# Fixed order on TensorE in the attention, later transposes, and the gains of q, k and v inside the split of their weights

## Chip, cores and metric

One core of one Trainium2 chip runs the whole program in one launch. The metric is the device time in microseconds (us) of an execution; the median of three runs of the kernel before is 1498.02 us (1497.49 to 1499.73). All data are float32, and the result is compared with a float32 reference.

## The reference

A trunk of two layers on 512 tokens of width 1024: a gated short convolution with its feed-forward part, then dilated attention with its own. The attention is what matters here. Keys and values come from a normalised stream with a gain of its own (`kv_norm`), queries from the same stream with `mix_norm_pre[1]`:

```
q = rope(rms_norm(x, mix_norm_pre[1]) @ w_q)       # 3 branches x 16 heads x 64
k, v = rms_norm(h, kv_norm) @ w_kv                 # the same split; k gets rope
for g, (window, dilation) in enumerate(((128, 1), (512, 4), (2048, 16))):
    s = (q_g / 8) @ k_g.T, masked to t, t-d, ..., t-window
    o_g = softmax(s) @ v_g ; lse_g = logsumexp(s)
o = sum_g softmax_g(lse) * o_g ; y = o @ w_o
```

## The kernel before, in words

Every large product is made of three matmuls on parts in a short float format: a weight w is split into `wh` (w rounded by ScalarE, `nc.scalar.copy` in `split`, L93) and `wl` (w minus `wh`, by VectorE, L94), an activation likewise into `xh`, `xl` (`zh`, `zl` are the same tiles seen in the attention's order), and `wh·xh + wl·xh + wh·xl` is summed in a PSUM bank. PSUM has eight banks, four with the tag "mm" and four with the tag "at". Weights arrive as 1 MB loads (L101, SyncE's queue, two `raw` tiles); a load gives two pairs of split tiles, and there are six tiles of each kind. For q, k and v the gain of the norm belongs to the rows of the weight, so `parts` first multiplies `raw` by it in place (L113, VectorE, two products for each half of a load) and then splits.

The attention goes through the 16 heads in four groups of four (`for i in range(NG)`, L758). A group has two stages.

- The q and k projections (`rope_mms`, L543): six loads, each a `feature_mm` of 48 matmuls of 512 columns into two "mm" banks, followed by `rope` (L527): eight ScalarE copies of 32x512 into two tiles of the pool "t" (four tiles), and three VectorE products for each bank. After each load `fill()` takes two pending pieces of work (L553).
- The v projections (`values`, L645): three loads in two pieces of 48 matmuls of 256 columns, and after each piece `fill()` again takes two.

What `fill` takes in the v stage are the scores (`scores`, L577): eight calls for two parts (branch 0; branches 1 and 2 together), two pairs of heads and two halves of the blocks. A call opens two "at" banks, and its matmuls use 64 rows of the array, rows 0 to 63 for one head of the pair and 64 to 127 for the other. VectorE adds the mask and takes the maximum (L597), ScalarE takes the exponential (L607). Then `factors` (L610) exchanges the sums of the two parts through DMAs on GpSimd's queue and makes one factor for each row. What `fill` takes in the following group's q and k stage are the units (L730): `transposed` (L676) scales p by its factor (VectorE, L685), transposes it into two "at" banks (L688) and lets ScalarE copy it into two tiles of the pool "t" (L690). One unit later `times_v` (L693) multiplies it with v into an "at" bank that two heads share (64 columns of the array each); the last one of a pair of heads copies that bank out on ScalarE (`O`, L726) or splits it into `xh`, `xl`. The last group's units stand between the first matmuls of the output projection (`wo_step`, L513; L781 to L784).

A planner with a simulated timeline makes each engine's order. It takes what is ready and was written first, gives out tiles of a pool as they are given back, and adds the waits. `tc.issue_after(m)` binds an instruction to come behind `m` on the same engine; before the change that is used in the attention only behind the first product with v (L716).

Of the kernel before, what the change touches and what calls it, by code (L numbers as in the profile page):

```python
# [7 lines left out]
F32 = mybir.dt.float32  # L8
# [30 lines left out]
def trunk(  # L39
# [64 lines left out]
    def parts(src, gain=None, pool=wp, bufs=6):  # L104

        _, a, b = src.shape
        wh = pool.tile([P, a, b], F32R, tag="wh", name="wh", bufs=bufs, align_bytes=LINE)
        wl = pool.tile([P, a, b], F32R, tag="wl", name="wl", bufs=bufs, align_bytes=LINE)
        if gain is not None:
            for i in range(0, a, a // 2):  # L110
                ks = slice(i, i + a // 2)
                g = gain[:, ks].rearrange("p (a x) -> p a x", x=1)
                nc.vector.tensor_tensor(  # L113
                    src[:, ks], src[:, ks], g.broadcast_to([P, a // 2, b]), ALU.mult)
        split(wh, wl, src)
        return wh, wl

# [4 lines left out]
    def feature_mm(jobs, t0, t1, attn):  # L122
# [28 lines left out]
    def feature_mms(makers, between=None, attn=False, marks=((),) * 4):  # L151
# [5 lines left out]
        if between is None:  # L157
            pairs = [m() for m in makers]
            for i in range(0, len(pairs), 2):
                feature_mm(pairs[i:i + 2], 0, NT, attn)  # L160
# [14 lines left out]
    def makers(tag, raw, gain=None):  # L175

        return [lambda j=j: (bank(tag, tag + "f"), parts(raw[:, :, j * P:(j + 1) * P], gain))
                for j in range(2)]

    def token_mm(outs, ah, al, wh, wl, first, last):  # L180

        for i, o in enumerate(outs):
# [330 lines left out]
    def wo_step(k, tt, n):  # L513
        wh, wl = ws[4 * n + k // 2]
        return token_mm([ys[tt][n]], xh[:, tt, k, :], xl[:, tt, k, :],
                        [wh[:, k % 2, :]], [wl[:, k % 2, :]], k == 0, k == KT - 1)

    with ExitStack() as inner:
# [24 lines left out]
        def rope_mms(g, i, rest, fill):  # L543
# [4 lines left out]
            for src, gain in ((w_q[0], gq), (w_kv, gkv)):  # L548
                tag = "at" if ms and rest else "mm"
                ms += makers(tag, load_cols(src, c0), gain)  # L550
                if not rest:
                    d += [rope(ps, f"qk{g}", g) for ps in feature_mms(ms[-2:], None, True)]
# [9 lines left out]
        class Heads:  # L562
# [14 lines left out]
            def scores(self, part, pr, b2):  # L577

                st = self.st[part]
                ps = [bank("at", "s").rearrange("p (b k) -> p b k", b=2) for _ in range(2)]  # L580
                for b in (b2, b2 + 1):
                    for e in range(2):
# [4 lines left out]
                        for h2 in range(2):  # L587
                            rw = slice(64 * h2, 64 * h2 + 64)
                            nc.tensor.matmul(  # L589
                                ps[h2][:, b - b2, e * P:(e + 1) * P],  # L590
                                q[pr][rw, b * P:(b + 1) * P], k[pr][rw, kb * P:(kb + 1) * P],
                                start=True, stop=True)
                    lo = 128 if part == 0 and b == 0 else 0
                    mask = (maskA, maskB)[part]
                    for h2 in range(2):
                        hh = 2 * pr + h2
                        nc.vector.tensor_tensor_reduce(  # L597
                            self.p(part, hh, b), ps[h2][:, b - b2, lo:], mask[:, lo:],
                            1.0, -3.0e38, ALU.add, ALU.max, st[:, b, hh, 0:1])
                if b2 == 0:  # L600
                    return
# [43 lines left out]
            def values(self, g):  # L645

                raw = load_cols(w_kv, QW + g * NH * HD + self.i * 256)
                w = [parts(raw[:, 4 * j:4 * j + 4, :], gkv[:, 4 * j:4 * j + 4]) for j in range(2)]
# [4 lines left out]
                def piece(n):  # L653
                    for k in range(KT):
                        wh, wl = (x[:, k % 4, :] for x in w[k // 4])
                        for p in range(3):
                            for m in range(2):
                                nc.tensor.matmul(  # L658
                                    ps[m][:, n, :], (zh, zh, zl)[p][:, k, 2 * m + n],
                                    (wh, wl, wh)[p],  # L660
                                    start=k == 0 and p == 0, stop=k == KT - 1 and p == 2)
# [14 lines left out]
            def transposed(self, pr, part, hh, b2):  # L676
# [5 lines left out]
                for b in (b2, b2 + 1):  # L682
# [4 lines left out]
                    for e in range(lo, 256, P):  # L687
                        nc.tensor.transpose(  # L688
                            tr[:, b - b2, e:e + P], p[:, e - lo:e - lo + P], ident)
# [3 lines left out]
            def times_v(self, pr, part, b2, trs):  # L693
# [5 lines left out]
                mark = None  # L699
                for b in (b2, b2 + 1):  # L700
                    for e in range(2):
                        if part == 0 and b + e == 0:
                            continue
                        for hh in range(2):
# [11 lines left out]
                            with tc.issue_after(mark) if mark else nullcontext():  # L716
                                m = nc.tensor.matmul(  # L717
# [146 lines left out]
```

## Time and profile before

| what | value |
|---|---|
| median of three runs | 1498.02 us |
| profiled execution | 1498.81 us, span 1497.0 us |
| TensorE (PE) | 1484.5 us busy, 99% |
| weight loads on TensorE (PEld) | 1256.2 us, 84% |
| VectorE (DVE) | 741.6 us, 50% |
| ScalarE (ACT) | 615.6 us, 41% |
| GpSimd (POOL) | 58.2 us, 4% |
| mean granted TensorE clock | 0.999 |
| HBM read, written | 133.92 MB, 2.23 MB |

An instruction's time runs from its start to its modelled end; matmuls overlap, so the distance from one start to the next is what one costs in a row of them. A run is what stands in one line of the timeline: instructions of one kind without another between them. One score matmul or product with v of the code is two instructions in the trace, one transpose is one.

### The profile page before, as it was taken

To read this page: it belongs to the slowest core of one execution; us is meant where nothing else is said; L and a number is where in the kernel's file an instruction comes from. 1 tells how busy PE (TensorE), PEld (TensorE's weight loads), DVE (VectorE), ACT (ScalarE), POOL (GpSimd) and SP (SyncE) were. 2 spreads that over 40 slices of the span, in tenths; PEclk is the share of its full clock that TensorE was granted. 3 is DMA by queue.
4 is the path that set the end of the run, shared out by engine and by line. 5 is a ranking of instruction groups with operands and counts; after the bars stand their busy time and mean duration, and the time that the engine had idled before them with its cause. 6 is when DMAs were issued, how large, how long until landed. Compare 5 with 4: busy or idle time off the path is not lost.

```text
span 1497.0 us, 19969 instructions
## 1 busy us (share of the span) xinstructions
PE 1484.5 (99%) x8155; PEld 1256.2 (84%) x8155; DVE 741.6 (50%) x1312; ACT 615.6 (41%) x1133; POOL 58.2 (4%) x108
## 2 busy tenths in 40 slices
PE   9999999999999999999999999999999999999998
PEld 8888898888888889898788889889879888888886
DVE  5735453323233368767667566765546332323332
ACT  5313342212123236574666557466554221212321
POOL 1000100000000020000001001000010000000000
PEclk9999999999999999999999999999999999999999
DMA  6343033223323303222122212212123322332311
GB/s 219 107 141 109 33 113 113 72 98 113 123 88 113 113 29 113 85 86 86 57 65 79 85 64 81 85 57 86 31 85 113 113 71 98 113 124 87 113 57 56
DMA packets 110369, 137.43 MB, mean 92 GB/s; under 512 B 3485, under 2 KB 99013, under 8 KB 110278
## 3 DMA queue, kind: packets, MB, share of 16 engines
q1 hardware_dynamic: 108708, 135.56, 27.2%
q8 instruction: 64, 1.05, 0.3%
q0 software_dynamic: 1280, 0.26, 0.2%
q10 hardware_dynamic: 290, 0.33, 0.1%
q14 instruction: 27, 0.22, 0.0%
HBM read 133.92 MB, written 2.23 MB: 91 GB/s over the span
## 4 chain that ended last, share of the span: by engine, by line
PE 66%; issue 26%; DMA 3%; DVE 2%; POOL 1%; ACT 1%; POOLq 0%; DVEq 0%; SPq 0%; ACTq 0%
PE mmf L140 26%; PE atf L140 14%; PE vps L658 8%; PE s L589 2%; PE o L717 2%; PE tr L688 2%; DMA raw<-in_w_kv 1%; DVE raw L113 1%; DMA raw<-in_ffn_w_gate_up 1%; POOL y L207 1%; DMA raw<-in_w_q 1%; DVE wl L94 1%; POOL a L205 1%; PE y1b L187 0%; PE y1a L183 0%
## 5 line engine op out<-in xcount | busy, mean ns | idle before, releaser
L94 DVE TENSOR_TENSOR wl<-raw,wh 128x1024 fp32r<-128x1024 f32 x244 | 292.9, 1222 | 74.6 <-ACT wh L93 74.2
L93 ACT CAST wh<-raw 128x1024 fp32r<-128x1024 f32 x244 | 246.8, 1047 | 104.3 <-PE atf L140 42.7
L140 PE MATMUL mmf<-xh,wh 128*128 128x512 f32 (+1 forms) x848 | 275.2, 377 | 2.8 <-ACT xh L93 2.8
L140 PE MATMUL mmf<-xl,wh 128*128 128x512 f32 (+1 forms) x848 | 271.4, 374 | 0.0
L140 PE MATMUL mmf<-xh,wl 128*128 128x512 f32 (+1 forms) x848 | 270.7, 374 | 0.0
L140 PE MATMUL atf<-xh,wh 128*128 128x512 f32 (+1 forms) x560 | 181.0, 365 | 0.0
L140 PE MATMUL atf<-xl,wh 128*128 128x512 f32 (+1 forms) x560 | 180.1, 365 | 0.0
L140 PE MATMUL atf<-xh,wl 128*128 128x512 f32 (+1 forms) x560 | 180.0, 365 | 0.0
L140 PEld LDWEIGHTS mmf<-xh,wh 128*128 128x128 f32 x848 | 152.8, 188 | 32.5 <-ACT xh L93 3.5
L366 DVE TENSOR_TENSOR act<-atf,s 128x512 f32<-128x512 f32 x44 | 30.4, 692 | 301.6 <-ACT s L365 301.6
L140 PEld LDWEIGHTS mmf<-xl,wh 128*128 128x128 f32 x848 | 153.3, 188 | 28.7 <-issue 0.9
L140 PEld LDWEIGHTS mmf<-xh,wl 128*128 128x128 f32 x848 | 153.3, 188 | 27.9
L365 ACT ACTIVATE s<-mmf 128x512 f32<-128x512 f32 x44 | 26.3, 598 | 334.9 <-PE mmf L140 326.7
L113 DVE TENSOR_TENSOR raw<-raw,cols 128x512 f32<-128x512 f32 x144 | 90.4, 686 | 85.7 <-DMA raw<-in_w_kv 60.5
L140 PEld LDWEIGHTS atf<-xl,wh 128*128 128x128 f32 x560 | 99.5, 189 | 16.9
L140 PEld LDWEIGHTS atf<-xh,wl 128*128 128x128 f32 x560 | 99.5, 189 | 17.0
L140 PEld LDWEIGHTS atf<-xh,wh 128*128 128x128 f32 x560 | 99.6, 188 | 16.6
L536 ACT COPY sw<-mmf 32x512 f32<-32x512 f32 x92 | 53.3, 579 | 78.7 <-PE mmf L140 71.4
L658 PE MATMUL vps<-wh,xh 128*128 128x256 f32 x384 | 81.2, 289 | 0.0
L658 PE MATMUL vps<-wh,xl 128*128 128x256 f32 x384 | 79.3, 286 | 0.0
L658 PE MATMUL vps<-wl,xh 128*128 128x256 f32 x384 | 79.1, 285 | 0.0
L94 DVE TENSOR_TENSOR al<-act,ah 128x512 fp32r<-128x512 f32 x44 | 30.2, 691 | 96.4 <-ACT ah L93 96.4
(182 smaller groups left out, 1993.6 us busy)
## 6 DMA issues: line engine op xcount, KB each, us to landing
raw<-in_ffn_w_gate_up SPq DMA_DIRECT2D x44, 1024.0 KB, 6.6
raw<-in_w_kv SPq DMA_DIRECT2D x24, 1024.0 KB, 5.2
raw<-in_ffn_w_down SPq DMA_DIRECT2D x22, 1024.0 KB, 4.8
raw<-in_w_q SPq DMA_DIRECT2D x12, 1024.0 KB, 5.2
raw<-in_conv_w_in SPq DMA_DIRECT2D x11, 1024.0 KB, 5.1
raw<-in_conv_w_out SPq DMA_DIRECT2D x4, 1024.0 KB, 4.8
raw<-in_w_o SPq DMA_DIRECT2D x4, 1024.0 KB, 5.0
h<-in_x SPq DMA_DIRECT2D x4, 512.0 KB, 7.1
```

Of the source, the lines that this page charges most:

```text
L93: return [nc.scalar.copy(hi, src).ins, nc.vector.tensor_tensor(lo, src, hi.bitcast(F32), ALU.subtract).ins]
L94: nc.vector.tensor_tensor(lo, src, hi.bitcast(F32), ALU.subtract).ins]
L113: nc.vector.tensor_tensor(src[:, ks], src[:, ks], g.broadcast_to([P, a // 2, b]), ALU.mult)
L140: nc.tensor.matmul(ps, (wh, wl, wh)[p][:, k, :], x[p == 2][:, k], start=i == 0, stop=i == len(todo) - 1)
L205: nc.gpsimd.tensor_scalar(a, ssq[:, 0:1], EPS, ssq[:, 1:2], ALU.add, ALU.add)
L365: nc.scalar.activation(s, ps[2 * j], AF.Silu)
L366: nc.vector.tensor_tensor(act[2 * c + j], ps[2 * j + 1], s, ALU.mult)
L536: nc.scalar.copy(w[s:s + 32], y[s + 32:s + 64])
L589: nc.tensor.matmul(ps[h2][:, b - b2, e * P:(e + 1) * P], q[pr][rw, b * P:(b + 1) * P], k[pr][rw, kb * P:(kb + 1) * P], start=True, stop=True)
L658: nc.tensor.matmul(ps[m][:, n, :], (zh, zh, zl)[p][:, k, 2 * m + n], (wh, wl, wh)[p], start=k == 0 and p == 0, stop=k == KT - 1 and p == 2)
L688: nc.tensor.transpose(tr[:, b - b2, e:e + P], p[:, e - lo:e - lo + P], ident)
L717: m = nc.tensor.matmul(out, v, rhs, start=first, stop=part == 0 and e == 1, skip_group_check=True).ins
```

## The change

The diff does three things. `strict` ties each of the attention's matmuls (q and k but for the first load pair, scores, v, transposes, products with v, the first 24 steps of the output projection) behind the one traced before it. The scores are four calls in place of eight, with four "at" banks each; `fill` takes one piece of work, before a v piece, and in a q or k load in the middle of its matmuls and behind its rope; the units come after three empty ones (but for the last group), and products with v of two units stand together. And `parts` with a gain makes `wh` by a ScalarE multiplication with a factor for each partition and `wl` by one VectorE instruction, one of each for each of the weight's 128-row slices, on half a load of 256 columns (`gained`); the product in place is gone.

```diff
     def parts(src, gain=None, pool=wp, bufs=6):
...
-        if gain is not None:
-            for i in range(0, a, a // 2):
-                ks = slice(i, i + a // 2)
-                g = gain[:, ks].rearrange("p (a x) -> p a x", x=1)
-                nc.vector.tensor_tensor(
-                    src[:, ks], src[:, ks], g.broadcast_to([P, a // 2, b]), ALU.mult)
-        split(wh, wl, src)
+        if gain is None:
+            split(wh, wl, src)
+            return wh, wl
+        for i in range(a):
+            g = gain[:, i:i + 1]
+            nc.scalar.mul(wh[:, i], src[:, i], g)
+            nc.vector.scalar_tensor_tensor(
+                wl[:, i], src[:, i], g, wh[:, i].bitcast(F32), ALU.mult, ALU.subtract)
         return wh, wl
 
+    def gained(raw, gain):
+        return [parts(raw[:, k:k + 4], gain[:, k:k + 4]) for k in (0, 4)]
...
+    traced = []
+    def strict(op, *args, **kwargs):
+        with tc.issue_after(traced[0]) if traced else nullcontext():
+            traced[:] = [op(*args, **kwargs).ins]
...
         for i, (k, p) in enumerate(todo):
-            for ps, (_, (wh, wl)) in zip(outs, jobs):
-                nc.tensor.matmul(ps, (wh, wl, wh)[p][:, k, :], x[p == 2][:, k],
-                                 start=i == 0, stop=i == len(todo) - 1)
+            if fill and i == len(todo) // 2:
+                fill()
+            for ps, (_, w) in zip(outs, jobs):
+                args = ps, w(p == 1, k), x[p == 2][:, k]
+                kwargs = {"start": i == 0, "stop": i == len(todo) - 1}
+                if fill:
+                    strict(nc.tensor.matmul, *args, **kwargs)
+                else:
+                    nc.tensor.matmul(*args, **kwargs)
...
-            def scores(self, part, pr, b2):
+            def scores(self, part, pr):
                 st = self.st[part]
-                ps = [bank("at", "s").rearrange("p (b k) -> p b k", b=2) for _ in range(2)]
-                for b in (b2, b2 + 1):
+                banks = [[bank("at", "s").rearrange("p (b k) -> p b k", b=2) for _ in range(2)]
+                         for _ in range(2)]
+                for b in range(NT):
...
-                w = [parts(raw[:, 4 * j:4 * j + 4, :], gkv[:, 4 * j:4 * j + 4]) for j in range(2)]
+                w = gained(raw, gkv)
...
-                def unit(pr, part, b2):
-                    self.flight.append(((pr, part, b2), [
-                        self.transposed(pr, part, hh, b2) for hh in (2 * pr, 2 * pr + 1)]))
-                    if len(self.flight) > 1:
+                def unit(n, what):
+                    if n % 2 == 0:
                         self.rest()
-                return [lambda a=(pr, part, b2): unit(*a)
-                        for pr in range(2) for part in (1, 0) for b2 in (0, 2)] + [self.rest]
+                    if what:
+                        pr, part, b2 = what
+                        self.flight.append((what, [
+                            self.transposed(pr, part, hh, b2) for hh in (2 * pr, 2 * pr + 1)]))
+                whats = [(pr, part, b2) for pr in range(2) for part in (1, 0) for b2 in (0, 2)]
+                return [lambda a=a: unit(*a) for a in enumerate(whats + [None])]
 
             def rest(self):
-                what, trs = self.flight.pop(0)
-                self.times_v(*what, trs)
+                for what, trs in self.flight:
+                    self.times_v(*what, trs)
+                self.flight.clear()
...
         def fill():
-            for f in todo[:2]:
-                f()
-            del todo[:2]
+            if todo:
+                todo.pop(0)()
...
-            todo = [lambda a=(part, pr, b2): heads.scores(*a)
-                    for part in range(2) for pr in range(2) for b2 in (0, 2)]
+            todo += [lambda a=(part, pr): heads.scores(*a)
+                     for part in range(2) for pr in range(2)]
             for g in range(NB):
                 for piece in heads.values(g):
+                    fill()
                     piece()
-                    fill()
             heads.factors()
-            todo = heads.units()
+            todo += [lambda: None] * (3 if i < NG - 1 else 0) + heads.units()
...
-        for n, f in enumerate(todo):
+        for n, f in enumerate(list(todo)):
             for s in steps[3 * n:3 * n + 3]:
-                wo_step(*s, 0)
+                wo_step(*s, 0, True)
             f()
```

## Rows read from the trace of the kernel before

**Rows 1.** Busy time by stretch: engines, granted clock, DMA share, GB/s.

```profile
624.90:673.60 48.70, 48.48 (x409) 44.80 (x408) 34.58 (x103) 35.06 (x98) 3.51 (x6) 1.00 0.28 88
673.60:756.50 82.90, 82.90 (x471) 66.93 (x470) 55.06 (x110) 45.14 (x76) 2.61 (x5) 1.00 0.23 72
756.50:803.90 47.40, 47.40 (x410) 44.30 (x409) 33.19 (x101) 34.42 (x97) 3.90 (x7) 1.00 0.25 78
803.90:885.90 82.00, 82.00 (x471) 66.64 (x470) 53.83 (x109) 45.13 (x75) 1.97 (x4) 1.00 0.24 75
...
1015.30:1062.80 47.50, 47.50 (x409) 44.16 (x408) 25.71 (x87) 36.78 (x100) 4.56 (x8) 1.00 0.22 75
1062.80:1101.40 38.60, 37.42 (x271) 29.46 (x269) 16.31 (x56) 15.91 (x30) 1.31 (x3) 1.00 0.09 29
```

**Rows 2.** Timeline of TensorE in a V stage: start, duration, instructions.

```profile
762.00 0.40 PE L658 MATMUL vps<-wh,xl 128*128 128x256 f32 x2
762.33 0.94 PE L589 MATMUL s<-qk,qk 64*128 64x128 f32 x12
763.20 0.50 PE L658 MATMUL vps<-wh,xh 128*128 128x256 f32 x2
763.54 0.39 PE L658 MATMUL vps<-wl,xh 128*128 128x256 f32 x2
...
777.35 1.16 PE L589 MATMUL s<-qk,qk 64*128 64x128 f32 x16
778.44 0.50 PE L658 MATMUL vps<-wh,xl 128*128 128x256 f32 x2
```

**Rows 3.** Timeline of TensorE in the QK stages.

```profile
690.43 0.61 PE L140 MATMUL mmf<-xh,wl 128*128 128x512 f32 x2
...
694.96 0.62 PE L140 MATMUL mmf<-xl,wh 128*128 128x512 f32 x2
...
815.25 1.91 PE L688 MATMUL tr<-ident,p 128*128 128x128 f32 x16
816.92 0.71 PE L140 MATMUL mmf<-xh,wl 128*128 128x512 f32 x2
...
825.72 1.09 PE L717 MATMUL o<-trs,v 128*64 128x128 f32 x16
826.75 0.73 PE L140 MATMUL mmf<-xl,wh 128*128 128x512 f32 x2
...
869.70 0.88 PE L717 MATMUL o<-trs,v 128*64 128x128 f32 x12
870.51 0.50 PE L140 MATMUL mmf<-xh,wh 128*128 128x512 f32 x1
```

**Rows 4.** Timeline of ScalarE behind two projections.

```profile
744.39 0.58 ACT L536 COPY sw<-mmf 32x512 f32<-32x512 f32 x1 [4.10 <-PE mmf L140]
...
749.13 2.00 ACT L93 CAST wh<-raw 128x1024 fp32r<-128x1024 f32 x2
751.15 0.59 ACT L726 COPY O<-o 128x512 f32<-128x512 f32 x1
...
819.51 2.00 ACT L93 CAST wh<-raw 128x1024 fp32r<-128x1024 f32 x2
821.53 1.08 ACT L690 COPY trs<-tr 128x512 f32<-128x512 f32 x2
```

**Rows 5.** Groups by line and shape: count, busy, mean ns, idle before.

```profile
L93 ACT CAST wh<-raw 128x1024 fp32r<-128x1024 f32 x244 | 246.8, 1047 | 104.3 <-PE atf L140 42.7 <-issue 14.0 <-DMA raw<-in_ffn_w_gate_up 14.0
L607 ACT ACTIVATE p<-p,nm 128x256 f32<-128x256 f32 x112 | 55.3, 496 | 11.7 <-DVE nm L604 9.9 <-DMA d<-st 1.8
...
L113 DVE TENSOR_TENSOR raw<-raw,cols 128x512 f32<-128x512 f32 x144 | 90.4, 686 | 85.7 <-DMA raw<-in_w_kv 60.5 <-DMA raw<-in_w_q 25.1
L464 DVE SCALAR_TENSOR_TENSOR conv<-u,cols,conv 128x512 f32<-128x512 f32 x16 | 11.3, 745 | 0.0
```

**Rows 6.** Timeline of ScalarE at the start of the output projection.

```profile
1065.28 1.05 ACT L666 COPY v<-vps 128x512 f32<-128x512 f32 x2
```

More of the change, by code (lines that the diff above doesn't have):

```diff
@@ L149, in behind, with feature_mms @@
             yield
-    def feature_mms(makers, between=None, attn=False, marks=((),) * 4):
+    def feature_mms(makers, between=None, attn=False, marks=((),) * 4, fill=None):
         half = NT // 2
@@ L159, in feature_mms @@
             for i in range(0, len(pairs), 2):
-                feature_mm(pairs[i:i + 2], 0, NT, attn)
+                feature_mm(pairs[i:i + 2], 0, NT, attn, fill)
             return [ps for ps, _ in pairs]
@@ L175, in makers, with make, token_mm @@
     def makers(tag, raw, gain=None):
-        return [lambda j=j: (bank(tag, tag + "f"), parts(raw[:, :, j * P:(j + 1) * P], gain))
-                for j in range(2)]
-    def token_mm(outs, ah, al, wh, wl, first, last):
+        ws = []
+        def make(j):
+            cs = slice(j * P, (j + 1) * P)
+            ps = bank(tag, tag + "f")
+            if gain is None:
+                w = parts(raw[:, :, cs])
+                return ps, lambda low, k: w[low][:, k, :]
+            if not ws:
+                ws.extend(gained(raw, gain))
+            return ps, lambda low, k: ws[k // 4][low][:, k % 4, cs]
+        return [lambda j=j: make(j) for j in range(2)]
+    def token_mm(outs, ah, al, wh, wl, first, last, strictly=False):
+        if strictly:
+            for i, o in enumerate(outs):
+                strict(nc.tensor.matmul, o, ah, wh[i], start=first, stop=False)
+                strict(nc.tensor.matmul, o, ah, wl[i], start=False, stop=False)
+                strict(nc.tensor.matmul, o, al, wh[i], start=False, stop=last)
+            return
         for i, o in enumerate(outs):
@@ L551, in rope_mms @@
                 if not rest:
-                    d += [rope(ps, f"qk{g}", g) for ps in feature_mms(ms[-2:], None, True)]
+                    d += [rope(ps, f"qk{g}", g) for ps in feature_mms(
+                        ms[-2:], None, True, fill=fill)]
                     fill()
@@ L588, in scores @@
                             rw = slice(64 * h2, 64 * h2 + 64)
[L589 to L592, printed above, removed]
+                            strict(nc.tensor.matmul,
+                                   banks[b // 2][h2][:, b % 2, e * P:(e + 1) * P],
+                                   q[pr][rw, b * P:(b + 1) * P], k[pr][rw, kb * P:(kb + 1) * P],
+                                   start=True, stop=True)
+                for b in range(NT):
                     lo = 128 if part == 0 and b == 0 else 0
@@ L657, in piece @@
                             for m in range(2):
[L658 to L661, printed above, removed]
+                                strict(nc.tensor.matmul,
+                                       ps[m][:, n, :], (zh, zh, zl)[p][:, k, 2 * m + n],
+                                       (wh, wl, wh)[p],
+                                       start=k == 0 and p == 0, stop=k == KT - 1 and p == 2)
                     if n:
@@ L715, in times_v @@
                             first = new and b == 0 and e == 0
-                            with tc.issue_after(mark) if mark else nullcontext():
-                                m = nc.tensor.matmul(
-                                    out, v, rhs, start=first, stop=part == 0 and e == 1,
-                                    skip_group_check=True).ins
-                            if first:
-                                mark = m
+                            strict(nc.tensor.matmul, out, v, rhs, start=first,
+                                   stop=part == 0 and e == 1, skip_group_check=True)
                 if part == 1 or b2 == 0:
```

21 lines of the change are left out of this document (9 added, 12 removed).

## Prediction

> **What bounds the kernel now.** I first cut the span into the stretches of the attention by TensorE's kinds of work [rows 1]. Four of them hold the projection of v with the scores between its pieces (V stages, one for each group of four heads: 48.7, 47.4, 47.4 and 47.5 us; the row of the third, like the second's, isn't shown). Three hold the projections of q and k for the next group together with the transposes and the products with v of the last one (QK stages: 82.9, 82.0, 82.0 us, the last not shown), and the last, 38.6 us, starts the output projection. The reader is to see two things there. TensorE is busy all of the time in the QK stages and in all but 0.2 us of the V stages, so no other engine holds it up; and VectorE and ScalarE are busy at most 36.8 us of a V stage, and 55.1 and 45.1 us of a QK stage. So what counts is how well TensorE's own queue is packed. A busy share can't show that, since a short instruction that follows one of another kind counts as busy too. I therefore read TensorE's timeline for the distance from one start to the next, first in a V stage [rows 2], then in the QK stages [rows 3]. Then I read ScalarE's timeline where its copies stand in line [rows 4], and the groups by line for the price of the weight split [rows 5].
>
> **Packing in a V stage.** Steady v matmuls start 0.24 us apart for each two, 0.12 each. A score matmul is two instructions, and its neighbour works in the other 64 rows: a run of 12 takes 0.87 us to the next v matmul (762.33 to 763.20), one of 16 takes 1.09. That is 0.055 an instruction and 0.21 a run; before the run 0.09 more passes than 0.24 (762.00 to 762.33), and the first v pair behind it takes 0.34, 0.10 more [rows 2]. So each run costs 0.40 us whatever its length. Now the runs have 2 to 16 instructions. After, each of the four calls of a group is one run, two of 28 and two of 32, in the order that pairs the row halves: 2 x (0.87 + 16 x 0.055) + 2 x (1.09 + 16 x 0.055) = 7.4 us, plus 4 x 0.19 at the borders, plus 288 v matmuls x 0.12 = 34.6: 42.8 us. Against the sum of the four stages, 191.0 [rows 1], 4 x 42.8 = 171.2 saves **19.8 us**.
>
> **Packing in a QK stage.** q and k matmuls start 4.53 us apart for 20 (690.43 to 694.96), 0.2265 each. Sixteen transposes take 1.67 us, 0.104 each; with something for the matmul behind a block, as at the other borders, I take 0.11 in blocks of any length. A run of 16 products with v takes 1.03, one of 12 takes 0.81, again 0.055 each, and I allow 0.15 at its borders [rows 3]. After, a group has 60 transposes and four runs of 28 or 32: 288 x 0.2265 = 65.2; 60 x 0.11 = 6.6; 2 x 1.91 + 2 x 1.69 + 4 x 0.15 = 7.8; in all 79.6. The three stages save 3.3 + 2.4 + 2.4 = 8.1, and the last stretch, with the same transposes and products, about 2.5: **10.6 us**. Packing is worth 30.4 us, if nothing waits. How much waits is the question, since now the planner fills every wait with other matmuls, and afterwards nothing in the chain may pass.
>
> **The wait that I expect: the first scores of a stage.** The twelve openings of a QK stage take three empty units and nine real ones, so the last products with v come right behind the last k matmul, and the first scores right behind them. A score call now opens four "at" banks at once, all there are, and one of them still holds those products until ScalarE has copied them (L726). Let k end at 0. The last products run to 1.7. The eight rope copies are queued first, and they need the tiles that the products' first half gives back at about 1.0 (the pool "t" has four, all held by transposed p). The eight take 4.74 us (744.39 to 749.13) [rows 4], so to 5.75; the copy of 0.6 then ends at 6.35, and the scores go on at 6.4. Their first two banks keep TensorE to 1.7 + 0.85 = 2.55. That is a wait of 3.9 us, at three of the four stages: **11.7 us lost**. Queued behind it on TensorE is everything: the rest of the scores and the whole v projection. Bounds: if the copy goes ahead of the rope, nothing; if the eight multiplications of a weight load (3.2 us, below) also go ahead, as two casts did at 749.13 [rows 4], 7.1 a stage, 21.3 in all. I take 3.9, since the rope is traced first and the copy next.
>
> **Smaller waits.** Before the output projection's third matmul group a bank must be copied out of v; that copy stood 2.5 us behind the start of the stretch (1065.28 against 1062.8) [rows 6], and only 1.4 us of matmuls come first, after which the order is fixed. With the copy of 0.5: 2 us, bounds 0 and 4. Transposes of every second odd unit need a bank that the unit before gives back when ScalarE has copied it. Today that copy came 4.6 us behind the end of its transposes (816.92 to 821.53), behind rope copies and two casts [rows 3, 4]; from one unit to the next pass 5.45 us (24 x 0.2265). So six such places lose 0 to 1.3 us each; I take 0.5, **3 us**. The three empty units cost nothing. Today the transposes begin 11.4 us into a QK stage (815.25 [rows 3] against 803.9), so the factors are there by then; after, the last scores stand three v pieces (17 us) before the stage's start and the transposes four openings (21.8 us) behind it.
>
> **The weight split.** Per load of q, k or v, ScalarE's two casts of 128x1024 (1.05) become eight multiplications of 128x256 with a factor from memory. The nearest row is the exponential of the same shape, which has an operand of that kind too: 0.496. Instructions in line overlap by about 0.1 (two casts of 1.05 end after 2.00) [rows 4, 5], so 0.40 each: 3.2 us in place of 2.0, bounds 2.0 and 4.0. VectorE loses four products of 0.686 and does eight subtractions with a factor, each below the 0.745 of the 128x512 form, about 0.45 [rows 5]. By V stage, with three loads: ScalarE 34.4 + 3 x 1.2 = 38.0 of 42.8; VectorE at most 33.2 - 8.2 + 10.8 = 35.8, even if the old subtractions are not taken off. Both stay under TensorE, and weights are split a load ahead, so this edit is worth 0 by itself; without that cover it would cost its 1.2 us a load, 36 loads, 43 us. No transfer is added or moved past another: SP's loads wait for a raw tile as now, until both engines have read it, and POOL's transfers of the factors follow scores that end earlier in their stage.
>
> The Trainium skill ("ScalarE: Activation LUTs", Rules for kernel authors) would give a plain multiplication to VectorE and not to ScalarE. By that rule the change puts the gain on the wrong engine, and the time is that of the third rival below. By the rows VectorE is the fuller one in a QK stage, 55.1 against 45.1, and neither limits, so the sum has nothing for it.
>
> **Sum.** 1498.8 (the profiled execution: span 1497.0 and 1.8 around it) - 30.4 + 11.7 + 2 + 3 = 1485.1. The median of the runs is 0.8 below that execution: **1484 us**.
>
> **Rivals.**
> 1. No wait at the first scores, because the copy out of the products' bank is queued ahead of the rope. For it: the copy is short and TensorE waits for it. Against: L726 came behind all eight and two casts [rows 4]. 1498.0 - 30.4 + 5 = 1473. Chance 0.22.
> 2. Only part of it packs: other matmuls still get into the runs, or more places of the fixed order wait a little, about 8 us more: 1492. Chance 0.10.
> 3. Slower: ScalarE's queue becomes what TensorE waits for, at the copies out of the banks. For it: the multiplications come on top, casts stood ahead of copies twice [rows 4], and V stages would fill 89% of ScalarE. The first scores then wait 7.1 us (21.3), the six transposes 1.3 (7.8), the output projection 4: 33 us, against 30.4 gained: 1501. It decides from a delay of some 3 us more per copy than I take. Against: today ScalarE idles before 744.39 for 4.1 us [rows 4]. Chance 0.10.
> 4. Slower: the scores don't pair in fixed order and cost 0.11 an instruction as transposes do: 480 x 0.055 = 26 us, 1510. Against: runs as long as 16 pair already [rows 2]. Chance 0.03.
> 5. The clock: TensorE at the lower of its levels (1.2 in place of 2.4 GHz) after each of the three waits. Every stretch has the full clock [rows 1], but in none did TensorE idle for long. At half clock a stretch of matmuls takes double its time; the gain of 13.7 is gone if each wait is followed by 9 us at half clock: about 1495 to 1500. Chance 0.05.
>
> The Trainium skill ("TensorE: Matmul & The Clock Gate", HAM oscillation) says that pauses between bursts of matmuls bring the half clock back. This trace can't tell, as it has no such pause.
>
> **How the numbers follow.** The forecast has 0.50: 1476 to 1491, by half the bounds of the first wait and of the small ones. What can be told from no change here is 0.2%, 3 us. Forecast and rivals 1 and 2 are faster, 0.82, with half of rival 5 (0.02); the rest of rival 5 is within; 3 and 4 are slower, 0.13. Range 1470 to 1497: it takes in the first two rivals and leaves out 3 and 4 and part of 5.
>
> **What would show it.** In the profile after: four scores runs per group and no shorter ones; V stages of 43 us in the first group and 47 in the others, where TensorE idles some 4 us before the second half of the first scores, until ScalarE's copy of the products; QK stages near 80 us; no row for the products of the weights on VectorE, and eight rows of 128x256 per load on each of the two engines. Wrong would be: a V stage longer than 50 us, score runs broken up, waits for transposed p of over 2 us at a time, or a clock below full.

## The result and the profile after

The changed kernel takes 1480.94 us (median of four runs, 1478.76 to 1484.23), against 1498.01 for the kernel before: ratio 0.9885, 95% interval 0.9873 to 0.9898. Forecast were 1484, in a range of 1470 to 1497. The profiled execution took 1481.55 us, span 1479.7, mean granted clock 0.998.

Busy time, engine by engine, from the page after: VectorE has lost 53 us and ScalarE gained 46, while TensorE is at 99% as before.

```profile
PE 1460.7 (99%) x8155; PEld 1247.2 (84%) x8155; DVE 689.0 (47%) x1384; ACT 661.1 (45%) x1349; POOL 57.2 (4%) x108
L116 DVE SCALAR_TENSOR_TENSOR wl<-raw,cols,wh 128x256 fp32r<-128x256 f32 x288 | 122.3, 481 | 109.6 <-ACT wh L115 109.6
L115 ACT ACTIVATE wh<-raw,cols 128x256 fp32r<-128x256 f32 x288 | 121.9, 498 | 70.3 <-PE mmf L133 46.7
```

The stretches of [rows 1] after the change, in the columns named there: the first V stage, the QK stage behind it, the second V stage, and the last stretch up to the last products with v.

```profile
630.05:672.75 42.70, 42.70 (x410) 41.82 (x409) 24.32 (x100) 38.09 (x115) 6.12 (x10) 1.00 0.28 90
672.75:752.61 79.86, 79.86 (x471) 66.33 (x469) 50.69 (x131) 54.55 (x115) 0.00 (x0) 1.00 0.25 80
752.61:796.36 43.75, 43.15 (x410) 42.10 (x409) 24.58 (x106) 36.40 (x116) 5.88 (x10) 1.00 0.26 75
...
1043.56:1080.95 37.39, 35.23 (x267) 27.90 (x265) 12.07 (x39) 12.76 (x24) 0.00 (x0) 1.00 0.08 28
```

A V stage takes 42.70 where nothing waits and 43.75 in the three groups where the first scores wait; the three QK stages 79.86, 79.84 and 79.85. From the start of the first V stage to the first matmul behind the last products TensorE now takes 450.9 us, before 474.3: 23.4 less. (The last stretch of [rows 1] reaches 2.2 us further, to 1101.4; by this measure it took 36.3 before.) But the span is only 17.3 shorter. TensorE's waits, longest first:

```profile
PE mmf L160 <- ACT xh L93: 4.3, 3, 2.8
PE s L133 <- DVE st L636: 1.8, 3, 0.6
PE tr L275 <- DVE hn L261: 1.6, 1, 1.6
...
PE y L133 <- ACT v L703: 1.2, 1, 1.2
```

The first row lies in the feed-forward part ahead of the attention, which the change leaves alone, and the third at the attention's opening. Together the stretch ahead of the first V stage is 5.2 us longer (630.05 against 624.89). The output's end behind the attention is 0.9 longer.

TensorE's timeline shows the runs: a V stage's run of 32 where [rows 2] had at most 16 (the four V stages have 16 runs in all, before 51), and the first scores of the second group, split in two by a wait of 0.60.

```profile
645.45 2.06 PE L133 MATMUL s<-qk,qk 64*128 64x128 f32 x32
647.44 0.50 PE L133 MATMUL vps<-wh,xh 128*128 128x256 f32 x2
...
750.93 1.75 PE L133 MATMUL o<-trs,v 128*64 128x128 f32 x28
752.61 1.16 PE L133 MATMUL s<-qk,qk 64*128 64x128 f32 x14
754.37 1.13 PE L133 MATMUL s<-qk,qk 64*128 64x128 f32 x14 [0.60 <-DVE st L636]
```

### The profile page after: what moved, and what is told of

It reads as the page before. It is cut to its first block, busy times and chain, and to the rows that moved or that the text cites. A ratio compares the mean times of both kernels' runs of the same rounds, so it can differ in the third digit from the quotient of the medians.

```text
span 1479.7 us, 20308 instructions
## 1 busy us (share of the span) xinstructions
PE 1460.7 (99%) x8155; PEld 1247.2 (84%) x8155; DVE 689.0 (47%) x1384; ACT 661.1 (45%) x1349; POOL 57.2 (4%) x108
## 4 chain that ended last, share of the span: by engine, by line
PE 67%; issue 28%; DVE 2%; POOL 1%; DMA 1%; ACT 1%; POOLq 0%; DVEq 0%; ACTq 0%; SPq 0%
PE mmf L133 16%; PE atf L160 14%; PE mmf L160 11%; PE vps L133 9%; PE s L133 2%; PE o L133 2%; PE tr L133 2%; PE y L133 1%; DMA raw<-in_ffn_w_gate_up 1%; POOL y L243 1%; POOL a L241 1%; DVE wl L116 1%; PE y0b L223 0%; PE y0a L221 0%; PE y0b L219 0%
## 5 line engine op out<-in xcount | busy, mean ns | idle before, releaser
L94 DVE TENSOR_TENSOR wl<-raw,wh 128x1024 fp32r<-128x1024 f32 x172 | 206.0, 1223 | 73.6 <-ACT wh L93 73.1
L93 ACT CAST wh<-raw 128x1024 fp32r<-128x1024 f32 x172 | 174.1, 1047 | 78.7 <-PE atf L160 42.7
L116 DVE SCALAR_TENSOR_TENSOR wl<-raw,cols,wh 128x256 fp32r<-128x256 f32 x288 | 122.3, 481 | 109.6 <-ACT wh L115 109.6
L160 PE MATMUL mmf<-xh,wh 128*128 128x512 f32 (+1 forms) x496 | 163.3, 366 | 4.3 <-ACT xh L93 4.3
L160 PE MATMUL mmf<-xl,wh 128*128 128x512 f32 (+1 forms) x496 | 160.6, 362 | 0.0
L160 PE MATMUL mmf<-xh,wl 128*128 128x512 f32 (+1 forms) x496 | 160.4, 362 | 0.0
L115 ACT ACTIVATE wh<-raw,cols 128x256 fp32r<-128x256 f32 x288 | 121.9, 498 | 70.3 <-PE mmf L133 46.7
L133 PE MATMUL mmf<-xh,wh 128*128 128x512 f32 x352 | 111.0, 396 | 0.0
L133 PE MATMUL mmf<-xh,wl 128*128 128x512 f32 x352 | 108.8, 390 | 0.0
L133 PE MATMUL mmf<-xl,wh 128*128 128x512 f32 x352 | 108.6, 390 | 0.0
L160 PEld LDWEIGHTS mmf<-xh,wh 128*128 128x128 f32 x496 | 89.3, 192 | 19.5 <-ACT xh L93 5.0
```

Source lines behind the costliest of these rows:

```text
L93: return [nc.scalar.copy(hi, src).ins, nc.vector.tensor_tensor(lo, src, hi.bitcast(F32), ALU.subtract).ins]
L94: nc.vector.tensor_tensor(lo, src, hi.bitcast(F32), ALU.subtract).ins]
L115: nc.scalar.mul(wh[:, i], src[:, i], g)
L116: nc.vector.scalar_tensor_tensor(wl[:, i], src[:, i], g, wh[:, i].bitcast(F32), ALU.mult, ALU.subtract)
L133: traced[:] = [op(*args, **kwargs).ins]
L160: nc.tensor.matmul(*args, **kwargs)
```

## Experiments

**The parts alone: split, chain, writing.** Three parts can carry the gain: the new weight split, the chain of `strict`, and the places at which scores and units are written. The first theory was the prediction's: the chain packs the runs.

e1, the kernel before with the new split only:

```diff
-        if gain is not None: ... (product in place), split(wh, wl, src)
+        for i in range(a):
+            nc.scalar.mul(wh[:, i], src[:, i], g)
+            nc.vector.scalar_tensor_tensor(wl[:, i], src[:, i], g, wh[:, i], MULT, SUBTRACT)
```

> The kernel before with only the new weight split (eight multiplications on ScalarE and eight fused subtractions on VectorE per load of q, k or v), TensorE's order as before. Theory A (packing carries the whole gain; the split is hidden but for the opening of the attention, where ScalarE and VectorE start the splits ahead of the norm's square and product): 0 to 3 us slower than before, 1498 to 1501, V stages of 47 to 48 us and QK stages of 82 as before. Rival B (the split frees VectorE, and that is where a good part of the gain comes from): 5 us or more faster, 1493 or less.

Measured: 1499.46 us (1497.96 to 1500.8), ratio 1.0005, 0.9996 to 1.0014: no change that can be told. The stages show that two things cancel. The four V stages take 186.2 us in all (191.1 before [rows 1]), but the first begins 2.3 us later (627.15 against 624.89), the three QK stages take 247.6 in all (246.9), and TensorE's other waits are longer. By these profiles, one of each kernel, the split is not free, and not worthless either.

e2, the changed kernel with the old split:

> The changed kernel with the old weight split (VectorE's product in place, then cast and subtraction), the fixed order kept. Theory A: all of the gain stays, and the 2 us that the new split cost at the attention's opening come back: 1478 to 1481, V stages of 42.7 and 43.7 us and QK stages of 79.9 as after. Rival B (the fixed order needs the lighter VectorE, whose mask additions and products stand ahead of what TensorE now may not pass): waits in the V or QK stages, 1486 or more.

Measured: 1479.89 (1479.80 to 1480.43), ratio 0.9877, 0.9864 to 0.9891. The first V stage begins at 624.68, so the opening's loss is gone. From there to the last products it takes 455.6 us, 4.7 more than the changed kernel: 1.7 in the V stages and 3.0 in the QK stages. TensorE's waits in e2:

```profile
PE s L132 <- DVE st L631: 3.6, 3, 1.2
...
PE o L132 <- ACT trs L722: 0.9, 2, 0.7
```

The waits at the first scores double: two subtractions of 128x1024 stand ahead of the call's mask additions on VectorE until 750.66, 1.56 us behind the call's start, where in the changed kernel the short ones are done 0.65 us behind it (753.26). Of the 3.0 us in the QK stages the waits for transposed p (the second row) show 0.9; the rest stays open. So the time is theory A's, and rival B is right in kind, not in size. What the new split is worth in the changed kernel can't be told from the times: e2 is 1.3 over the second measurement of the changed kernel (e12 below, 1478.64) and 1.1 under the first (1480.94). The profiles show what stands against what: 4.7 us gained inside the attention, and 2.3 lost at its opening (the first V stage of e12 begins at 626.95). The Trainium skill ("ScalarE: Activation LUTs", Rules for kernel authors) would have had the product stay on VectorE; inside the attention these rows speak for ScalarE here, because VectorE's queue gives the banks back, and at its opening for VectorE.

e3, the changed kernel without the chain:

```diff
     def strict(op, *args, **kwargs):
-        with tc.issue_after(traced[0]) if traced else nullcontext():
-            traced[:] = [op(*args, **kwargs).ins]
+        return op(*args, **kwargs).ins
```

> The changed kernel without the chain that fixes TensorE's order: the same work written at the same places, with the same later transposes, and the planner free to place it. Theory A (the chain packs the runs): the score runs fall apart again, V stages of 46 to 48 us and QK stages of 81 to 82, 18 us or more slower than after, 1496 to 1502. Rival B (the place at which the work is written gives most of the packing): within 5 us of after, 1481 to 1486.

Measured: 1479.32 (1478.17 to 1480.06), ratio 0.9872, 0.9858 to 0.9885. Theory A falls. Without the chain the stages are as good as with it: only the first call of three groups is in two runs, of 20 and 8, and the V stages there take 43.97 for 43.75, the QK stages 79.92 for 79.85. The last stretch is better, 36.25 against 37.39:

```profile
751.54:795.51 43.97, 43.97 (x411) 42.83 (x409) 24.58 (x106) 36.42 (x116) 5.88 (x10) 1.00 0.26 75
...
1043.28:1079.53 36.25, 35.58 (x266) 28.80 (x264) 12.13 (x39) 12.67 (x24) 0.00 (x0) 1.00 0.04 13
```

So theory C: the writing does it. The next three runs take it apart.

e5, the kernel before with the scores alone written as in the change:

```diff
-    for b in (b2, b2 + 1):        # two banks; per block: matmuls, then its mask additions
+    for b in range(NT):           # four banks; all matmuls of the call
...
+    for b in range(NT):           # then all mask additions
```

> The kernel before with the scores alone written as in the change: four calls with four banks each, all matmuls of a call ahead of its mask additions, one call after each of the first four v pieces. No chain, the old split, the QK stages as before. The run without the chain had the whole gain, so theory C: the way the scores are written packs the V stages. Then these fall from 47.5 to 43 to 44 us, some 15 us in all: 1481 to 1485. Rival D (the planner needs the freer VectorE of the new split, or the call ahead of its v piece, to do it): score runs still broken up, V stages of 46 us or more, 1492 to 1498.

Measured: 1489.62 (1487.27 to 1491.28), ratio 0.9942, 0.9928 to 0.9955. The V stages do what theory C says: 42.77 us, in whole runs, without the chain and with the old split. In all four 19.5 us are gone. The time lies between the two theories all the same, since the QK stages give 5.4 us of it back and the last stretch 2.0. The second V stage and the QK stage behind it:

```profile
750.50:793.27 42.77, 42.77 (x409) 41.75 (x408) 29.32 (x96) 31.54 (x89) 2.94 (x5) 1.00 0.27 88
793.27:878.71 85.44, 82.47 (x470) 66.49 (x469) 56.78 (x114) 47.69 (x84) 2.95 (x5) 1.00 0.22 71
```

In the QK stages 4.5 us are the wait of the first transposes for their factors (2.97 here, 1.54 in the third), in TensorE's timeline of e5:

```profile
807.31 2.20 PE L688 MATMUL tr<-ident,p 128*128 128x128 f32 x16 [2.97 <-DVE p L685]
```

Shorter V stages leave the factors less time. The last mask addition of the V stage ahead stands at 790.42, 2.9 us before that stage ends, and VectorE scales p only from 806.16. What covers this in the full change is not the later units: e9 below has its first transposes as early (at 801.74, 10.9 us into the QK stage) and no wait, since there the last mask addition stands at 775.88, 15.0 us before the stage's end. Two things bring it forward, the call ahead of its v piece and the shorter split; no run parts them. The forecast for e5, 1481 to 1485, missed this.

e6, the kernel before with the units alone written as in the change:

```diff
-            todo = heads.units()
+            todo += [lambda: None] * (3 if i < NG - 1 else 0) + heads.units()
...
+            if fill and i == len(todo) // 2:
+                fill()
```

> The kernel before with the units alone written as in the change: three empty ones first, one unit at each opening, openings also in the middle of a load's matmuls, products with v of two units together. No chain, the old split, the scores as before. Theory C (the writing packs the QK stages too): QK stages of 80 us, V stages of 47 to 48, 7 to 10 us faster than before: 1488 to 1491. Rival D (the planner takes the pieces apart again without the chain): 1495 to 1498.

Measured: 1495.95 (1494.73 to 1499.3), ratio 0.9985, 0.9977 to 0.9994. The QK stages fall to 80.4, but the second and third V stage rise to 49.1, with their runs still broken up:

```profile
753.44:802.57 49.13, 48.97 (x411) 45.09 (x410) 30.95 (x97) 33.00 (x97) 4.89 (x9) 1.00 0.21 66
802.57:883.00 80.43, 80.43 (x470) 66.37 (x468) 56.99 (x114) 46.46 (x76) 1.00 (x2) 1.00 0.25 79
```

The time is rival D's, but theory C holds for the QK stages. Alone the two writings are worth 8.5 and 2.2 us; in e3, with the new split and the call ahead of its v piece, 18.7.

e7, the kernel before with the chain alone, everything written as before:

> The kernel before with the chain alone: scores, units and openings written as before, but TensorE keeps to the written order in the attention. Theory C (the chain is not what gains): the runs are as long as they are written, 28 or 32, but two score calls stand right behind each other with banks that VectorE's mask additions have to give back, and each product with v stands one unit behind its transposes, so that TensorE idles more than 5 us in all: 1486 or more, perhaps slower than before. Rival A (fixing the order is the gain, wherever the work stands): 1479 to 1484.

Measured: 1669.56 (1666.8 to 1671.65), ratio 1.1143, 1.1128 to 1.1158: 171 us slower: theory C's side, but far more than it expected. TensorE's waits and, below, the first two score calls (12 and 16 instructions) of its first V stage:

```profile
PE s L127 <- DVE st L612: 48.1, 33, 4.9
PE tr L127 <- ACT trs L705: 43.4, 9, 4.9
PE o L127 <- ACT trs L705: 16.4, 3, 5.5
```

```profile
630.73 0.49 PE L127 MATMUL s<-qk,qk 64*128 64x128 f32 x4
636.11 0.79 PE L127 MATMUL s<-qk,qk 64*128 64x128 f32 x2 [4.89 <-DVE st L612]
637.46 3.82 PE L127 MATMUL s<-qk,qk 64*128 64x128 f32 x22 [0.56 <-DVE st L612]
```

This shows one way in which the old writing breaks a run. Four instructions, block 0 of two heads, and then TensorE waits for a mask addition of its own call. The first ends at 636.05 and the next two instructions go at 636.11; the second lies at 637.11 to 637.39 and the rest goes at 637.46:

```profile
635.77 0.28 DVE L612 CUSTOM_DVE_ANT_0 p<-s,cst 128x128 f32<-128x128 f32 x1
...
637.11 0.28 DVE L612 CUSTOM_DVE_ANT_0 p<-s,cst 128x128 f32<-128x128 f32 x1
```

Two blocks share a bank. Written block by block, the second block's matmuls come behind the first block's mask additions, and on VectorE these stood behind the old split of a weight (631.61 to 635.25) and a sum of the rope (to 635.84). The Trainium skill ("PSUM — Partial Sum Buffer", PSUM bank collisions raise a hardware error) says that TensorE may not write a bank that VectorE reads at that time, even in other columns of it. The rows agree: with two blocks in one bank, TensorE's next write to it waits for VectorE's read. With the mask additions written behind all matmuls of a call (e5) the wait is gone.

For the kernel before this is a part only. Free to choose, the planner put this very call into one run, its mask additions behind it (from 636.50). Others it broke, with v matmuls between the pieces. From TensorE's timeline of the kernel before:

```profile
630.73 0.94 PE L589 MATMUL s<-qk,qk 64*128 64x128 f32 x12
...
783.12 0.71 PE L589 MATMUL s<-qk,qk 64*128 64x128 f32 x4
...
785.15 1.16 PE L589 MATMUL s<-qk,qk 64*128 64x128 f32 x12
```

Between the last two lies a mask addition of the same call (784.48). Counted in order through the four V stages, 18 of the 32 calls are one run each and 14 are broken into 33 pieces; 10 of these 14 have two of their own mask additions between their first and last matmul. So of the 35 runs by which 51 became 16, 19 were breaks inside calls and 16 were borders between calls that are now one. e5 takes away both at once, and no run parts the two.

The idle time of the three rows of waits is 108 us. The lower granted clock of these stages (last section) adds to it: over the 646.1 us from the first V stage to the last products it was 0.87 on the mean, which is worth 84 us at most (an estimate: 0.13 of that time, idle time included). It was not measured apart.

**The opening, the parity, and what could still be had.** e4 binds k's first split behind ScalarE's square of y3b and VectorE's product behind it, and q's for the next branch behind the last normed tile:

```diff
+    def first(self):
+        rest = self.rest()
+        rest["marks"][2] = rest["marks"][2] + self.marks[NT - 1]
+        return rest
...
+    if i == 0 and g == 1 and gain is gq:
+        ms[-2:] = [lambda m=m: late(m) for m in ms[-2:]]   # behind marks and normed of NT - 1
```

> The changed kernel with one more binding: at the opening of the attention the first split of k waits for ScalarE's square of y3b and VectorE's product behind it, and that of q for the last normed tile, so that the splits no longer stand ahead of the norm. Theory A (the split's queueing ahead of the norm cost 2 us there): TensorE's idle 1.6 us at the transposes that wait for hn goes, 1479 to 1480, 1 to 2 us faster than after. Rival B (the norm is late anyway, or the split then comes late for the k matmuls behind it): 1481 to 1483, the wait only moves.

Measured: 1476.73 (1476.15 to 1480.8), ratio 0.9861, 0.9848 to 0.9875; 1.9 under e12, which ran on another chip. The two ratios don't part them (e12: 0.9862), since one of e4's four runs took 1480.80; the trace does. In ScalarE's and then VectorE's timeline of the changed kernel the split stands ahead of the norm: twelve multiplications ahead of the square (in e4 it starts at 556.74, right behind the matmuls), and fourteen subtractions ahead of hn, for which TensorE idles 1.58 us.

```profile
557.51 4.91 ACT L115 ACTIVATE wh<-raw,cols 128x256 fp32r<-128x256 f32 x12 [1.21 <-PE y3b L223]
562.32 0.57 ACT L235 ACTIVATE junk<-y3b 128x512 bf16<-128x512 f32 x1
```

```profile
565.40 5.62 DVE L116 SCALAR_TENSOR_TENSOR wl<-raw,cols,wh 128x256 fp32r<-128x256 f32 x14
...
572.94 0.87 DVE L261 TENSOR_SCALAR hn<-h,y 128x512 f32<-128x512 f32 x2
```

In e4 hn starts at 566.15 (in e12, where the late load doesn't shift it, at 569.84), and TensorE's wait for it is gone; the first V stage begins at 625.39, in e12 at 626.95. Theory A holds in the trace, with a time below its forecast.

e8, e4 with two empty units in place of three:

> The changed kernel with the binding at the attention's opening of the run e4, and two empty units in place of three, so that the last products with v no longer stand right ahead of the first scores. Theory A (the 1.06 us at three of the four first scores is the bank that the mask additions of the same call give back, because the products' bank is the fourth): all three go, 1473 to 1474, no wait of the scores for st. Rival B (an opening earlier the transposes wait for their factors): 1476 or more, with TensorE idle at the first transposes of a QK stage.

Measured: 1498.01 (1497.74 to 1502.42), ratio 1.0003: the whole gain lost by one `None`. The wait of the first scores is gone, and all V stages take 42.70, as theory A says. But the QK stages take 88.2, by neither theory:

```profile
PE o L133 <- ACT trs L740: 18.8, 12, 1.6
```

ScalarE's timeline of e8 shows the queue:

```profile
694.99 0.58 ACT L579 COPY sw<-mmf 32x512 f32<-32x512 f32 x1
695.59 1.71 ACT L115 ACTIVATE wh<-raw,cols 128x256 fp32r<-128x256 f32 x4
697.33 0.59 ACT L740 COPY trs<-tr 128x512 f32<-128x512 f32 x1
697.81 1.71 ACT L115 ACTIVATE wh<-raw,cols 128x256 fp32r<-128x256 f32 x4
699.42 0.57 ACT L740 COPY trs<-tr 128x512 f32<-128x512 f32 x1
```

Openings alternate between the middle and the end of a load. With an even number of empty units a pair's second transposes fall on the end, where eight rope copies and four multiplications stand ahead of the first copy that the products need, and four more ahead of the second. That is the prediction's third rival, at another place: a QK stage takes 88.2 in place of e9's 80.1, 2.0 us for each of its four products, of which 1.6 are idle.

e9 takes one empty unit (`* (1 if ...)`), e10 is e9 without the chain, e11 is e9 with ScalarE's casts of heads 1, 3 and 5 bound behind the last v copies, and e12 is the changed kernel again.

> As the run e8, but one empty unit in place of two. In e8 TensorE waited 1.6 us at each product with v, because the second transposes of a pair fell on the end of a load, where eight rope copies and four multiplications stand ahead of their copy on ScalarE. With an odd number of empty units the products fall there, as in the changed kernel, and one load earlier, away from the first scores. Theory A (only the parity and the fourth bank matter): no wait of the products for trs, none of the first scores for st, 3.2 us less than the run e4: 1473 to 1474. Rival B (a load earlier the factors aren't there): TensorE idles at the first transposes of a QK stage, by the waits of the run e5 up to 3 us each, 1476 to 1480.

> The kernel of e9 without the chain on TensorE. Theory C (the places at which the work is written do it all): within 2 us of e9, 1472 to 1476. Rival A (here, with fewer empty units, the planner breaks the runs up, since more of them find their data late by its reckoning): 5 us or more slower than e9.

> The kernel of e9 with one binding more: ScalarE's casts of the heads 1, 3 and 5 for the output projection stand behind its copies of the last v. In the changed kernel three such casts (3.1 us) stood ahead of these copies, and TensorE idled 1.24 us for the bank. Theory: 1.2 us less than e9, 1472 to 1473, no wait of y for v. Rival: the casts are then late for the products behind, and the wait only moves.

> The changed kernel once more, on the same chip as e9 to e11. Theory: 1480 to 1481 again; the 2.9 us that its first profile lost ahead of the attention, in code that the change leaves alone, belong to single executions (a weight load that landed 1.6 us later), so a second profile need not show them. Rival: they come with this program every time, and the profile shows them again.

| run | median, us | range | ratio to before, interval |
|---|---|---|---|
| e9 | 1473.70 | 1473.48 to 1478.32 | 0.9843, 0.9823 to 0.9862 |
| e10 | 1472.48 | 1472.33 to 1472.90 | 0.9821, 0.9806 to 0.9836 |
| e11 | 1473.46 | 1472.77 to 1475.63 | 0.9830, 0.9813 to 0.9846 |
| e12 | 1478.64 | 1478.33 to 1479.25 | 0.9862, 0.9847 to 0.9877 |

e9: theory A holds, V stages of 42.70 and no wait of scores or transposes; a QK stage takes 80.09. e10: theory C again, and it beats both kernels, by 6.2 us the changed one on the same chip (e12). Its V stages take 42.70 too; its last stretch:

```profile
1036.41:1072.67 36.26, 35.59 (x267) 28.80 (x265) 12.13 (x39) 12.68 (x24) 0.00 (x0) 1.00 0.04 15
```

The difference to e9 is the last stretch, 36.26 against 37.38, where the chain waits. e11: its rival is right, the wait moves. v comes in time, and TensorE idles for an `xl` instead:

```profile
PE y L133 <- DVE xl L94: 1.3, 1, 1.3
```

e12: the first V stage begins at 626.95, not 630.05, and ScalarE's cast of the late weight load starts at 203.93 where the first profile had 205.72. So 3 us of that first profile belong to that execution. What makes the load late in some runs stays open.

## Why the prediction was right, and where not

The time fell into the range, 3 us under the forecast. By the prediction's terms, for the profiled execution (the split's share is e1's):

| term | predicted | measured |
|---|---|---|
| packing, V stages | -19.8 | -20.3 (191.1 to 4 x 42.70) |
| packing, three QK stages | -8.1 | -7.3 |
| packing, last stretch | -2.5 | -0.4, without its waits |
| wait at the first scores | +11.7 | +3.2 (3 x 1.06) |
| transposes' banks | +3 | 0 |
| output projection's start | +2 | +1.5 (1.24, and 0.25 for p) |
| split at the opening | 0 | +2.3 |
| ahead of the attention, behind it | 0 | +2.9, +0.9 |

The measured column sums to -17.2; the spans differ by 17.3. That the total came so near is in part luck. The forecast sum was -13.7: its waits were 12.0 us too long, and against that stand 2.4 us of packing that did not come and 6.1 us of the last two rows, which it had put at nothing.

**Packing.** For whole runs the price, 0.40 us whatever the length, was right: 42.8 forecast for a V stage, 42.70 measured. For the short runs of the kernel before it is too low. The twelve score runs of its second V stage take 10.6 us, each counted to the next v matmul, where 0.055 an instruction and 0.21 a run give 9.1. The saving was taken from the stage's own 47.4, which holds this. The reason for the packing was wrong. The step "now the planner fills every wait with other matmuls, and afterwards nothing in the chain may pass" is true of e7, where it costs 171 us. But the chain isn't what packs (e3, e10). What made the runs short was the writing: twice the calls, and in part of them a wait for the mask additions of a block of the same call (e7), which the new `scores` doesn't have. The whole diff shows that they move, and the prediction passed over it. In the last stretch there was little to pack: its products came in runs of up to 28 already (1096.59).

**The first scores.** The failed step is "one of them still holds those products until ScalarE has copied them". ScalarE's queue went nearly as forecast: four multiplications (751.04 to 752.75), eight rope copies, and the copy 6.57 us behind the end of k (forecast 5.75).

```profile
752.77 0.58 ACT L572 COPY sw<-mmf 32x512 f32<-32x512 f32 x1
...
757.50 0.59 ACT L758 COPY O<-o 128x512 f32<-128x512 f32 x1
```

But nobody waited for it: the second half of the scores went at 754.37, behind the second mask addition, whose maximum was read out at 754.14. That is the instruction whose signal TensorE waits for here:

```profile
753.58 0.29 DVE L636 CUSTOM_DVE_ANT_0 p<-s,cst 128x128 f32<-128x128 f32 x1 [0.32 <-PE s L133]
...
753.79 0.42 DVE L636 CUSTOM_DVE_ANT_0 p<-s,cst 128x256 f32<-128x256 f32 x1
754.14 0.08 DVE L636 DVE_READ_ACCUMULATOR2_ANT st<- 128x1 f32 x1
```

The reading that fits is that the call's fourth bank was its own first one, free once its two blocks had been read by these two mask additions. A broken run then adds its price: 0.60 of the 1.06 us are idle time. In e9, with the products a load earlier, all of it is gone.

**The split.** "Worth 0 by itself" holds for steady stages: ScalarE, forecast at 38.0 us of a V stage, took 38.1 in the first and 36.4 in the second. (The forecast went by the second stage of [rows 1]; the first and last had more, 35.1 and 36.8 before the change.) It failed at the attention's opening, which the prediction didn't look at, and it didn't see that the first scores make VectorE's queue count (e2).

**Rivals.** The first (no wait, 1473) is what e9 reaches, by another way than it said. The second did not come: the runs stayed whole but for three, and the other waits stayed small. The third, ScalarE's queue, did not come either, but e8 shows how near it is. Nor did the fourth: a run of 32 takes 1.99 us to the next matmul (645.45 to 647.44), so the scores pair. The fifth, the clock, did not come in the attention.

## What to carry to other kernels

Before fixing an engine's order, look in the written order for a wait inside each group. Where two blocks share a PSUM bank and the reader of one is written ahead of the writer of the other, the run can break there. Writing two such groups as one, with the readers behind all writers, gained most here (e5; which of the two did more was not parted). A fixed order is worth no more than the order that it fixes: on the old one it cost 171 us, on the new one it gained nothing. And count what else falls on the same opening: one empty unit more or less moved 24 us (e8 against e9).

## What the hardware showed beside this

After an idle time TensorE's granted clock fell in some places and not in others. In the changed kernel's first profile the late load left TensorE idle for 2.77 us (to 207.30), and the clock was at the lower level, 0.50 (1.2 of 2.4 GHz), for the 3.41 us from 206.88:

```profile
203.80:206.88 3.08, 0.73 (x7) 0.49 (x5) 0.26 (x2) 1.16 (x2) 0.00 (x0) 1.00 0.03 11
206.88:210.29 3.41, 2.99 (x14) 2.99 (x15) 2.34 (x3) 2.14 (x3) 0.00 (x0) 0.50 0.00 0
```

In e5 an idle time of 2.97 us (to 807.31) left it at full speed:

```profile
803.00:807.31 4.31, 1.34 (x6) 0.79 (x6) 2.90 (x21) 2.45 (x8) 0.00 (x0) 1.00 0.23 76
807.31:809.00 1.69, 1.69 (x13) 1.37 (x14) 1.69 (x8) 1.64 (x4) 0.00 (x0) 1.00 0.00 0
```

The same pause can go either way. The wait of 1.58 us for hn at the attention's opening left the clock at 1.00 in the changed kernel and was followed by 3.41 us at 0.50 in e3, whose code is the same there; that costs e3 some 1.7 of the 2.0 us by which its first V stage begins later than e12's (628.91 against 626.95). The changed kernel behind the wait, then e3:

```profile
573.47:577.00 3.53, 3.29 (x25) 3.06 (x26) 1.63 (x3) 1.08 (x2) 0.00 (x0) 1.00 0.92 301
```

```profile
572.16:575.57 3.41, 3.41 (x16) 3.41 (x17) 1.26 (x2) 0.43 (x1) 0.00 (x0) 0.50 0.68 235
```

In e7, with waits of up to 4.9 us, a V stage had 0.79 on the mean:

```profile
624.89:699.10 74.21, 59.45 (x409) 55.75 (x408) 36.40 (x108) 35.47 (x98) 6.13 (x10) 0.79 0.19 58
```

The twelve waits of 1.6 us in e8 left the mean clock at 0.999. The kernel before had a pause too, where the prediction saw none: 1.41 us ahead of the attention (to 205.75), at 1.00 throughout. Part of the spread of the runs goes with the clock: e9 took 1473.48 to 1473.70 us where its mean was 0.999 or more, and 1477.74 and 1478.32 where it was 0.996 and 0.997. The Trainium skill ("TensorE: Matmul & The Clock Gate", HAM oscillation) says that pauses between bursts bring the lower clock back; e7 bears that out, and the rows of e3, e5 and e8 show that not every pause of this kernel does and that its length alone does not decide.
